# A two-layer attention trunk: readback of the transposed weights in a later step, and output blocks taken in another order

## The chip, the cores and the metric

The kernel runs on one core of a Trainium2 chip. The metric is the device time of one execution in microseconds (us), lower is better. One more execution was recorded by the hardware profiler; every row below is from it, with times counted from the start of its span. The granted clock of TensorE was 0.999 of full speed, which is the 2.4 GHz level, over the whole span.

## What is computed

256 tokens of width 2048 pass through two residual layers in float32. Layer a is multi-head latent attention, layer b is causal attention with ALiBi (its block selection has nothing to select at 256 tokens). Both have 16 heads of width 128, a gate, and an output projection. Cut to what matters:

```python
# layer a: h = rms_norm(x, norm_a)
proj = h @ w_in                        # 2048 -> 512 + 256 + 64 + 2048
q_lat, kv_lat, k_rope, gate = split(proj)
q  = rms_norm(q_lat) @ w_q_up          # 16 heads x (128 + 64 rotary)
kv = rms_norm(kv_lat) @ w_kv_up        # 16 heads x (128 key + 128 value)
q, k = rms_norm per head, rope on the rotary parts (one rotary key for all heads)
o = softmax(causal(q @ k.T * scale)) @ v
x = x + (o * silu(gate)) @ w_out_a     # 2048 -> 2048
# layer b: h = rms_norm(x, norm_b)
q, k, v, gate = split(h @ w_in_b)      # 4 x 2048
o = softmax(causal(rms_norm(q) @ rms_norm(k).T * scale - slope * distance)) @ v
x = x + (o * silu(gate)) @ w_out_b
```

## The kernel before

**Products.** A float32 product is made of three products of rounded halves: high by high, high by low, low by high. A weight tile (128 partitions by up to 1024 columns, `wr`, 512 KB) is loaded by SyncE's queue, its high half `wh` is made by ScalarE (L147), its low half `wl` by VectorE (L151), and TensorE multiplies (L199). There are four buffers of `wr`, four of `wh` and three of `wl`, taken in turn. TensorE's transposes are L202. Five of the eight banks of PSUM hold sums of blocks (`acc`), three serve the heads (`ps_s` for scores, `ps_o` for P·V, `ps_ta` for turned tokens, `ps_st` and `ps_r` for token statistics).

**Layer a.** After the latent projections, eight groups of two heads follow one another (`group_a`, L656 to L745), each with its part of w_q_up, of w_kv_up, and a gate block. A head is made of steps (`head_steps`, L450): the scores and softmax (`s1`: minimum L464, exponential L466, norm L469 and L471); the turning of the probabilities, which are split into two planes by ScalarE (L441), transposed by a DMA on SyncE's queue (L442), and put together again by VectorE, the *readback* (L448 in `flip`); their high half `ph` and low half `pl` (L490 and L493 on ScalarE, L491 on VectorE); and P·V (`s3`) with its gating L505 and the halves of the result, `ohl` (L506 on ScalarE, L507 on VectorE). If `away` is set, the turning stops behind the DMA, and the readback (L483) with the halves is a step of its own, later. Layer b's heads have `away=FLB` before and after the change.

The output projection of layer a is eight blocks of 256 columns, `outs_a`, each of 16 steps; step i needs head i. Blocks 0 to 3 use one bank and six matmuls of 256 columns a step, blocks 4 to 7 two banks and four matmuls (two of 512 and two of 256 columns). When a block ends, VectorE adds it to x (L406), ScalarE and VectorE split the new x (L333, L334) and sum its squares (L346, L348, L350, L351). Before that x and the causal mask's place in `c_sb` are loaded again (`reload`): four loads of xT and, last, the ALiBi distances, from which ScalarE makes each head's `alibi` tile in layer b (L883, L882 after the change).

**Layer b.** Four groups of four heads (`group_b`, L825), each with a gate (two blocks of 16 steps), q, k and v. Its token statistics are two small products, `ps_st` and `ps_r`; ps_r needs a diagonal from VectorE (L370).

**What sets the order.** `ordered` (L168) merges a main list (blocks of products) and a side list (head steps, turns, reloads). Each step has a planned cost, things it needs, and a lag behind them; a side step goes out as soon as its planned time has come. `run` then writes out the steps, with each load four weights ahead. Each engine works its instructions in order; a framework between the kernel and the engines may still set independent instructions of one engine in another order. TensorE's order is fixed by `chain`.

Of the kernel before, what the change touches and what calls it, by code (L numbers as in the profile page):

```python
# [31 lines left out]
NC = DM // P  # L32
# [12 lines left out]


PA, PB, LO, TU, TUB, S1, S2A, S2B, S3 = 9000, 6000, 5000, 3000, 10000, 4800, 6000, 9000, 3000
FLB = 4500
SLACK = 1.3
HOLD = 4500  # L50
PACE, PACEB = 600, 3500
# [42 lines left out]
def trunk(ctx: ExitStack, tc, xT, gains, cst, w_in_a, w_q_up, w_kv_up, w_out_a, w_in_b, w_out_b, outT):  # L94
    nc = tc.nc
# [422 lines left out]
    main, side = [], []  # L518
# [137 lines left out]
    def group_a(g):  # L656
# [65 lines left out]
        def scores(h):  # L722
            def f(ps):
                at = lambda x, i: [y[:, i] for y in x]
                products(ps, at(z["q"], h), at(z["k"], h), True)
                products(ps, at(z["r"], 0), at((krf,) + lat_st["kr"], h), False)
            return f
# [5 lines left out]
        for h in range(2):  # L733
            heads.append(head_steps(2 * g + h, scores(h), lambda: c_sb[:, C_MASK:C_MASK + 384],
                                    lambda h=h: [x[:, h] for x in z["v"]], 1090, turns + [kr], [], gates[g][-1:],
                                    S2A, nc.scalar.copy))
        proj[0].needs += lats
        if g > 1:
            proj[-1].after += turns_of[-2]
# [35 lines left out]
    def out_done_a(j):  # L775
        def f(a):
            xt = res["x"]
            c = 2 * j
            added(a, xt, c)
            split_x(c, G_NB)  # L780
            split_x(c + 1, G_NB)
            sum_squares(ssq_b, j)
        return f
# [9 lines left out]
    outs_a = [(blk_cols if j < 4 else blk_both)(w_out_a[:, 256 * j:256 * (j + 1)], og, out_done_a(j), 4000) for j in range(8)]  # L793

    for g in range(8):
        main += group_a(g)
        if g == 0:
            kr.after.append(main[-1])
        if g < 7:
            main += gates[g + 1][HALF:] + (gates[g + 2][:HALF] if g < 6 else [])  # L800
        gates[g][-1].after.append(row_a)
        if g > 3:
            gates[g][-1].after += [h[2] for h in heads[2 * g - 8:2 * g - 6]]
# [10 lines left out]
            outs_a[2 * j][-1].needs.append(again)  # L814
    for b in outs_a[:4]:
        main += b[:12]
    for b in outs_a[:4]:
        main += b[12:]
    main += sum(outs_a[4:], [])


    x_b = x_a
# [2 lines left out]
    def group_b(g):  # L825
# [49 lines left out]
        def scores(h):  # L875
            def f(ps):
                products(ps, [x[:, h] for x in z["Q"]], [x[:, h] for x in z["K"]], True)
            return f

        def bias(h):  # L880
            def f():
                b = wk.tile([P, 384], F32, tag="alibi", name="alibi", bufs=1)  # L882
                nc.scalar.activation(b, c_sb[:, C_MASK:C_MASK + 384], AF.Copy,  # L883
                                     scale=float(np.float32(2.0 ** (-8.0 * (h + 1) / H))))
                return b
            return f

        w = lambda i: w_in_b[:, DM * i + 512 * g:DM * i + 512 * (g + 1)]
        gate = []
# [9 lines left out]
        for h in range(4):  # L899
            hb.append(head_steps(4 * g + h, scores(h), bias(4 * g + h), lambda h=h: [x[:, h] for x in z["v"]],  # L900
                                 545, [tq, tk], v[-1:] + gate[-1:], [], S2B, nc.vector.tensor_copy, PACEB if g < 3 else PACE, FLB))
        for s in (gate[NC - 1], gate[-1]):
# [8 lines left out]
        turns_of.extend([[tq], [tk]])  # L911
        side.extend([tq, tk])
        side.extend(s for h in hb[-4:] for s in h)
        return gate + q + k + v

    def out_done_b(c0, m):
# [14 lines left out]
    for g in range(4):  # L931
        main += group_b(g)
# [66 lines left out]
```

## Time and profile before

| what | us |
|---|---|
| median of 3 runs | 754.15 (752.91 to 754.26) |
| the profiled execution | 752.38 |
| its span, first to last instruction | 750.6 |
| TensorE busy | 740.6 (99%) |
| VectorE busy | 589.5 (79%) |
| ScalarE busy | 491.3 (65%) |
| DMA, mean | 204 GB/s |

The table says how much of the span each engine worked. It does not say which wait matters; that is read from who waits for whom, from the chain of work that ended last, and from the timelines of single stretches. Layer a's groups lie between about 75 and 250 us, its output blocks end by 310 us, and layer b fills the rest.

### The profile page before, as it was taken

What the parts mean: (1) busy time and instruction counts of PE and PEld (TensorE: products, weight loads), DVE (VectorE), ACT (ScalarE), POOL (GpSimd) and SP (SyncE); (2) the same over time, 40 slices, a digit from 0 to 9 for tenths busy, and PEclk for the clock granted to TensorE, in tenths of its full rate; (3) what the DMA queues carried; (4) which work ended last, traced back from release to release, by engine and by line L of the source; (5) the groups of instructions that cost most, each with busy time, mean ns of one, the idle gap of its engine ahead of it and who ended that gap; (6) DMA issues with size and microseconds to landing.
All of it is one profiled execution on the core that took longest, in us unless ns stands there. A gap on an engine that the chain in (4) does not pass through costs nothing.

```text
span 750.6 us, 13198 instructions
## 1 busy us (share of the span) xinstructions
PE 740.6 (99%) x4766; PEld 689.4 (92%) x4766; DVE 589.5 (79%) x1244; ACT 491.3 (65%) x1041; POOL 0.2 (0%) x4
## 2 busy tenths in 40 slices
PE   8999999999999999999999999999999999999997
PEld 7999999999999989988889988898889988899997
DVE  6978899999998696775788867887787967878563
ACT  7767888888877575555666666675666766565441
POOL 0000000000000000000000000000000000000000
PEclk9999999999999999999999999999999999999999
DMA  9866666666666966667787868877779778867761
GB/s 301 268 177 183 169 185 162 180 177 153 189 180 180 294 196 221 198 181 210 222 223 210 205 197 225 230 201 205 208 227 220 200 212 223 215 214 201 249 221 49
DMA packets 150258, 153.13 MB, mean 204 GB/s; under 512 B 47280, under 2 KB 119344, under 8 KB 150192
## 3 DMA queue, kind: packets, MB, share of 16 engines
q1 hardware_dynamic: 150048, 152.27, 71.6%
q8 instruction: 37, 0.61, 0.3%
q14 instruction: 29, 0.24, 0.1%
q10 hardware_dynamic: 144, 0.02, 0.0%
HBM read 139.68 MB, written 2.10 MB: 189 GB/s over the span
## 4 chain that ended last, share of the span: by engine, by line
PE 90%; DVE 5%; DMA 2%; ACT 1%; issue 1%; SPq 0%; DVEq 0%; ACTq 0%
PE acc L199 83%; PE ps_s L199 4%; DVE wl L151 3%; PE ps_o L199 2%; PE ps_ta L202 1%; DMA c_sb<-cst 1%; DMA wr<-w_in_a 1%; ACT wh L147 1%; DMA sm<-pz 0%; DVE xt L406 0%; ACT sq L598 0%; ACT sf L584 0%; DVE rs_y L328 0%; DVE rs_t L327 0%; PE ps_lt L202 0%
## 5 line engine op out<-in xcount | busy, mean ns | idle before, releaser
L147 ACT ACTIVATE wh<-wr 128x1024 fp32r<-128x1024 f32 (+3 forms) x265 | 288.4, 1092 | 143.1 <-PE acc L199 116.6
L151 DVE TENSOR_TENSOR wl<-wr,wh 128x1024 fp32r<-128x1024 f32 (+3 forms) x265 | 314.1, 1189 | 72.3 <-PE acc L199 41.8
L199 PE MATMUL acc<-wh,xhl 128*128 128x512 f32 (+1 forms) x896 | 265.6, 375 | 0.9 <-ACT wh L147 0.9
L199 PEld LDWEIGHTS acc<-wh,xhl 128*128 128x128 f32 x896 | 169.0, 190 | 21.7 <-ACT wh L147 1.5
L199 PE MATMUL acc<-xhl,wh 128*128 128x256 f32 (+1 forms) x768 | 173.4, 313 | 0.0
L199 PE MATMUL acc<-ohl,wh 128*128 128x256 f32 (+1 forms) x800 | 172.2, 307 | 0.0
L199 PE MATMUL acc<-wl,xhl 128*128 128x512 f32 (+1 forms) x448 | 167.8, 375 | 0.8 <-DVE wl L151 0.8
L199 PE MATMUL acc<-ohl,wl 128*128 128x256 f32 x512 | 140.7, 275 | 0.6 <-DVE wl L151 0.6
L199 PE MATMUL acc<-xhl,wl 128*128 128x256 f32 x512 | 140.3, 274 | 0.0
L199 PEld LDWEIGHTS acc<-ohl,wh 128*128 128x128 f32 x800 | 130.1, 191 | 6.0
L199 PEld LDWEIGHTS acc<-xhl,wh 128*128 128x128 f32 x768 | 126.5, 191 | 6.5
L199 PEld LDWEIGHTS acc<-ohl,wl 128*128 128x128 f32 x512 | 98.4, 192 | 1.3 <-DVE wl L151 1.2
L199 PEld LDWEIGHTS acc<-xhl,wl 128*128 128x128 f32 x512 | 98.4, 192 | 0.2
L199 PEld LDWEIGHTS acc<-wl,xhl 128*128 128x128 f32 x448 | 85.0, 190 | 11.6 <-DVE wl L151 1.6
L199 PE MATMUL acc<-wh,xt 128*128 128x384 f32 (+1 forms) x192 | 57.3, 356 | 0.0
L466 ACT ACTIVATE sm<-sm,mn 128x128 f32<-128x128 f32 x64 | 29.1, 457 | 12.9 <-DVE mn L464 12.9
L199 PEld LDWEIGHTS acc<-wh,xt 128*128 128x128 f32 x192 | 35.1, 190 | 1.2
L199 PE MATMUL acc<-wl,xt 128*128 128x384 f32 (+1 forms) x96 | 33.6, 350 | 1.5 <-DVE wl L151 1.5
L406 DVE TENSOR_TENSOR xt<-acc,xt 128x256 f32<-128x256 f32 (+1 forms) x37 | 16.1, 484 | 14.1 <-PE acc L199 14.1
L490 ACT CAST ph<-pz 128x256 fp32r<-128x256 f32 x32 | 12.9, 403 | 18.8 <-DVE pz L483 10.6
L507 DVE TENSOR_TENSOR ohl<-og,ohl 128x256 fp32r<-128x256 f32 x32 | 13.5, 424 | 12.2 <-ACT ohl L506 11.7
L506 ACT ACTIVATE ohl<-og 128x256 fp32r<-128x256 f32 x32 | 13.8, 433 | 12.8 <-DVE og L505 12.7
(150 smaller groups left out, 724.9 us busy)
## 6 DMA issues: line engine op xcount, KB each, us to landing
wr<-w_in_b SPq DMA_DIRECT2D x128, 512.0 KB, 4.0
wr<-w_in_a SPq DMA_DIRECT2D x32, 512.0 KB, 4.1
wr<-w_out_a SPq DMA_DIRECT2D x32, 512.0 KB, 4.5
wr<-w_out_b SPq DMA_DIRECT2D x32, 512.0 KB, 4.4
wr<-w_in_a SPq DMA_DIRECT2D x15, 416.0 KB, 5.0
wr<-w_q_up SPq DMA_DIRECT2D x16, 384.0 KB, 3.8
wr<-w_kv_up SPq DMA_DIRECT2D x8, 512.0 KB, 4.0
xt<-xT SPq DMA_DIRECT2D x4, 512.0 KB, 5.2
```

The source lines that it names most:

```text
L147: nc.scalar.activation(self.ordering(self.h)[1], self.ordering(self.raw)[0], AF.Copy)
L151: nc.vector.tensor_tensor(self.ordering(self.l)[1], self.ordering(self.raw)[0], self.ordering(self.h.bitcast(F32))[1], op=ALU.subtract)
L199: chain(nc.tensor.matmul(*args, skip_group_check=True, **kw))
L202: chain(nc.tensor.transpose(*args))
L406: nc.vector.tensor_tensor(lines(y), unpaired(b[:, o:o + n]), lines(y), op=ALU.add)
L466: nc.scalar.activation(sm[:, sl], sm[:, sl], AF.Exp, bias=mn[:, t:t + 1], scale=-1.0, accum_out=rs[:, t:t + 1])
L490: nc.scalar.copy(ph, pz[:, :S])
L506: nc.scalar.activation(lines(ogh[:, h]), unpaired(og), AF.Copy)
L507: nc.vector.tensor_tensor(lines(ogl[:, h]), unpaired(og), lines(ogh[:, h].bitcast(F32)), op=ALU.subtract)
```

## The change

Three things. In groups 1 to 5 of layer a (heads 2 to 11) `away` is set to 4000, so that the planes are copied and transposed at a lag of 4000 behind the scores instead of 6000, and read back (L483) in a step of its own at a lag of 2000 behind that. The last four steps of output blocks 0 to 3, which stood together, are set between halves of blocks 4 and 5. In layer b's first group the first four steps of the second gate block are set before the last four of the first.

```diff
--- before.py
+++ after.py
@@ -45,7 +45,7 @@
 
 
 PA, PB, LO, TU, TUB, S1, S2A, S2B, S3 = 9000, 6000, 5000, 3000, 10000, 4800, 6000, 9000, 3000
-FLB = 4500
+FLA, FLB = 4000, 4500
 SLACK = 1.3
 HOLD = 4500
 PACE, PACEB = 600, 3500
@@ -733,7 +733,7 @@
         for h in range(2):
             heads.append(head_steps(2 * g + h, scores(h), lambda: c_sb[:, C_MASK:C_MASK + 384],
                                     lambda h=h: [x[:, h] for x in z["v"]], 1090, turns + [kr], [], gates[g][-1:],
-                                    S2A, nc.scalar.copy))
+                                    S2A, nc.scalar.copy, away=FLA if 0 < g < 6 else 0))
         proj[0].needs += lats
         if g > 1:
             proj[-1].after += turns_of[-2]
@@ -814,9 +814,8 @@
             outs_a[2 * j][-1].needs.append(again)
     for b in outs_a[:4]:
         main += b[:12]
-    for b in outs_a[:4]:
-        main += b[12:]
-    main += sum(outs_a[4:], [])
+    o = outs_a
+    main += o[0][12:] + o[4][:8] + o[1][12:] + o[4][8:] + o[2][12:] + o[5][:8] + o[3][12:] + o[5][8:] + o[6] + o[7]
 
 
     x_b = x_a
@@ -911,6 +910,8 @@
         turns_of.extend([[tq], [tk]])
         side.extend([tq, tk])
         side.extend(s for h in hb[-4:] for s in h)
+        if g == 0:
+            gate = gate[:12] + gate[NC:NC + 4] + gate[12:NC] + gate[NC + 4:]
         return gate + q + k + v
 
     def out_done_b(c0, m):
```

Rows of the instruction order are shown for three places. Numbers behind names tell buffers apart: `wl_3103` is the low half of the weight loaded as `wr_3099`.

VectorE around the readbacks of heads 10 (first `pz`) and 11 (second `pz`), before:

```order
L448 COPY pz_3015<-sm_2924 128x2x384
L151 TENSOR_TENSOR wl_3035<-wr_2991,wh_2993 128x768
L491 TENSOR_TENSOR pl_3020<-pz_3015,ph_3019 128x256
L394 TENSOR_TENSOR gx_3072<-acc_2734,rr_a_590 128x512
L151 TENSOR_TENSOR wl_3080<-wr_3031,wh_3033 128x1024
L448 COPY pz_3049<-sm_2950 128x2x384
L396 SCALAR_TENSOR_TENSOR gate_3071<-gate_3071,gx_3072 128x512
L151 TENSOR_TENSOR wl_3110<-wr_3076,wh_3078 128x1024
L491 TENSOR_TENSOR pl_3054<-pz_3049,ph_3053 128x256
L427 SCALAR_TENSOR_TENSOR sr0_3097<-ps_ta_3098,gq_a_119,sr0_3097 128x256
L151 TENSOR_TENSOR wl_3162<-wr_3106,wh_3108 128x1024
```

and after:

```order
L394 TENSOR_TENSOR gx_3058<-acc_2720,rr_a_590 128x512
L151 TENSOR_TENSOR wl_3066<-wr_3024,wh_3026 128x1024
L396 SCALAR_TENSOR_TENSOR gate_3057<-gate_3057,gx_3058 128x512
L483 COPY pz_3015<-sm_2924 128x2x384
L151 TENSOR_TENSOR wl_3103<-wr_3062,wh_3064 128x1024
L491 TENSOR_TENSOR pl_3084<-pz_3015,ph_3083 128x256
L427 SCALAR_TENSOR_TENSOR sr0_3090<-ps_ta_3091,gq_a_119,sr0_3090 128x256
L151 TENSOR_TENSOR wl_3162<-wr_3099,wh_3101 128x1024
L427 SCALAR_TENSOR_TENSOR sr0_3090<-ps_ta_3111,g_sb_70,sr0_3090 128x512
L483 COPY pz_3042<-sm_2950 128x2x384
L505 SCALAR_TENSOR_TENSOR og_3154<-ps_o_3149,gate_2361 128x256
L491 TENSOR_TENSOR pl_3144<-pz_3042,ph_3143 128x256
```

Head 10's readback moved behind a gate product, a weight's low half and the gate; head 11's readback and `pl` moved behind two more low halves and both L427 of the next group, and head 10's P·V result (L505) comes between.

ScalarE at the end of layer a, where `og_3763` is head 15 before:

```order
L147 ACTIVATE wh_3677<-wr_3675 128x1024 [waits DMAHW2_49,PE_49]
L147 ACTIVATE wh_3708<-wr_3706 128x1024 [waits DMAHW5_49,PE_49]
L506 ACTIVATE ohl_74<-og_3723 128x256 [waits DVE_49]
L147 ACTIVATE wh_3748<-wr_3746 128x1024 [waits DMAHW7_49,PE_49,Activation_49]
L506 ACTIVATE ohl_74<-og_3763 128x256 [waits DVE_49]
L883 ACTIVATE alibi_5151<-c_sb_71 128x384 [waits DMAHW3_49]
L147 ACTIVATE wh_3787<-wr_3785 128x1024 [waits DMAHW0_49,PE_49,Activation_49]
```

and after, where `og_3781` is head 15:

```order
L147 ACTIVATE wh_3747<-wr_3745 128x1024 [waits DMAHW6_49,PE_49]
L506 ACTIVATE ohl_74<-og_3741 128x256 [waits DVE_49]
L147 ACTIVATE wh_3787<-wr_3785 128x1024 [waits DMAHW0_49,PE_49,Activation_49]
L882 ACTIVATE alibi_5151<-c_sb_71 128x384 [waits DMAHW3_49]
L506 ACTIVATE ohl_74<-og_3781 128x256 [waits DVE_49]
L147 ACTIVATE wh_3826<-wr_3824 128x1024 [waits DMAHW2_49,PE_49,Activation_49]
```

The tile `alibi`, which waits for the reload of `c_sb`, stood behind the halves of head 15 (second L506) and now stands in front of them; one more `wh` went in front of both.

VectorE in the updates of the output blocks, where before `acc_3375`, `acc_3559` and `acc_3681` are blocks 1, 2 and 3:

```order
L406 TENSOR_TENSOR xt_3673<-acc_3375,xt_3673 128x512
L151 TENSOR_TENSOR wl_3867<-wr_3824,wh_3826 128x1024
L334 SCALAR_TENSOR_TENSOR xhl_73<-xt_3673,g_sb_70,xhl_73 128x256 x2
L350 TENSOR_TENSOR ssq_125<-ssq_125,sq_3859 128x256
L406 TENSOR_TENSOR xt_3673<-acc_3559,xt_3673 128x512
L351 TENSOR_TENSOR ssq_125<-ssq_125,sq_3859 128x256
L151 TENSOR_TENSOR wl_3907<-wr_3863,wh_3865 128x1024
L334 SCALAR_TENSOR_TENSOR xhl_73<-xt_3673,g_sb_70,xhl_73 128x256 x2
L350 TENSOR_TENSOR ssq_125<-ssq_125,sq_3898 128x256
L406 TENSOR_TENSOR xt_3673<-acc_3681,xt_3673 128x512
```

and after, where `acc_3830` and `acc_3831` are block 4 and `acc_3548` is block 2:

```order
L151 TENSOR_TENSOR wl_3937<-wr_3910,wh_3912 128x1024
L351 TENSOR_TENSOR ssq_125<-ssq_125,sq_3906 128x256
L406 TENSOR_TENSOR xt_3698<-acc_3830,xt_3698 128x256
L406 TENSOR_TENSOR xt_3698<-acc_3831,xt_3698 128x256
L406 TENSOR_TENSOR xt_3698<-acc_3830,xt_3698 128x256
L406 TENSOR_TENSOR xt_3698<-acc_3831,xt_3698 128x256
L151 TENSOR_TENSOR wl_3971<-wr_3933,wh_3935 128x1024
L334 SCALAR_TENSOR_TENSOR xhl_73<-xt_3698,g_sb_70,xhl_73 128x256 x2
L350 TENSOR_TENSOR ssq_125<-ssq_125,sq_3963 128x256
L406 TENSOR_TENSOR xt_3698<-acc_3548,xt_3698 128x512
```

Blocks 1, 2 and 3 were added one after the other; now block 4's four additions, a low half and block 4's split stand before the addition of block 2, whose bank block 5 takes next.

## Rows read from the trace of the kernel before

**Rows 1.** The page: busy time, share; a group: busy and mean ns | idle, releaser.

```profile
PE 740.6 (99%) x4766; PEld 689.4 (92%) x4766; DVE 589.5 (79%) x1244; ACT 491.3 (65%) x1041; POOL 0.2 (0%) x4
...
L490 ACT CAST ph<-pz 128x256 fp32r<-128x256 f32 x32 | 12.9, 403 | 18.8 <-DVE pz L483 10.6
```

**Rows 2.** Waits of TensorE, whole span: us in total, times, longest us.

```profile
PE acc L199 <- DVE wl L151: 2.9, 9, 0.6
```

**Rows 3.** TensorE's timeline, heads 10/11: start us, us, engine, line, shapes [idle before].

```profile
210.40 0.27 PE L199 MATMUL ps_o<-ph,vh 128*128 128x256 f32 x1
210.51 0.28 PE L199 MATMUL ps_o<-pl,vh 128*128 128x256 f32 x1
...
212.04 0.38 PE L199 MATMUL acc<-wh,xt 128*128 128x512 f32 x1
212.27 0.38 PE L199 MATMUL ps_o<-ph,vh 128*128 128x256 f32 x1
```

**Rows 4.** TensorE's timeline, kv_up of group 1.

```profile
123.97 0.46 PE L199 MATMUL acc<-wh,xt 128*128 128x512 f32 x1
124.70 0.48 PE L199 MATMUL acc<-wl,xt 128*128 128x512 f32 x1 [0.27 <-DVE wl L151]
```

**Rows 5.** The chain of waits, layer a: start us, us, what.

```profile
190.38 1.14 DVE wl L151
...
228.68 3.31 DMA sm<-pz
...
251.83 8.17 DMA c_sb<-cst
```

**Rows 6.** VectorE's timeline, heads 10 and 11.

```profile
209.16 0.61 DVE L448 COPY pz<-sm 128x768 uint16<-128x768 uint16 x1
...
211.39 0.42 DVE L491 TENSOR_TENSOR pl<-pz,ph 128x256 fp32r<-128x256 f32 x1
...
212.12 1.22 DVE L151 TENSOR_TENSOR wl<-wr,wh 128x1024 fp32r<-128x1024 f32 x1
213.26 0.75 DVE L427 SCALAR_TENSOR_TENSOR sr<-ps_ta,g_sb,sr 128x512 fp32r<-128x512 f32 x1
```

**Rows 7.** Waits of VectorE, 80 to 250 us: us in total, times, longest.

```profile
DVE pz L448 <- DMA sm<-pz: 4.2, 7, 1.4
```

**Rows 8.** TensorE's timeline, scores of head 14.

```profile
232.73 0.36 PE L199 MATMUL ps_s<-sr 128*128 128x256 f32 x1
233.31 0.51 PE L199 MATMUL ps_s<-sr 128*128 128x256 f32 x2 [0.22 <-DVE sr L427]
```

**Rows 9.** ScalarE's timeline, end of layer a.

```profile
256.10 0.43 ACT L506 ACTIVATE ohl<-og 128x256 fp32r<-128x256 f32 x1
260.02 0.52 ACT L883 ACTIVATE alibi<-c_sb 128x384 f32<-128x384 f32 x1 [3.49 <-DMA c_sb<-cst]
```

**Rows 10.** TensorE's timeline, blocks 0 and 4 of layer a's output.

```profile
257.20 0.39 PE L199 MATMUL acc<-ohl,wh 128*128 128x256 f32 x2
...
268.53 0.38 PE L199 MATMUL acc<-ohl,wh 128*128 128x512 f32 x1
269.20 0.38 PE L199 MATMUL acc<-ohl,wl 128*128 128x256 f32 x1 [0.29 <-DVE wl L151]
```

**Rows 11.** VectorE's timeline, block 0's update.

```profile
258.07 0.69 DVE L406 TENSOR_TENSOR xt<-acc,xt 128x512 f32<-128x512 f32 x1
```

**Rows 12.** VectorE's timeline, update of a block in two banks.

```profile
287.88 1.42 DVE L406 TENSOR_TENSOR xt<-acc,xt 128x256 f32<-128x256 f32 x4 [1.01 <-PE acc L199]
289.21 1.22 DVE L151 TENSOR_TENSOR wl<-wr,wh 128x1024 fp32r<-128x1024 f32 x1
290.34 0.88 DVE L334 SCALAR_TENSOR_TENSOR xhl<-xt,g_sb,xhl 128x256 fp32r<-128x256 f32 x2
```

**Rows 13.** TensorE's timeline, layer b's token statistics.

```profile
319.13 0.27 PE L199 MATMUL acc<-xhl,wl 128*128 128x256 f32 x1
319.88 0.81 PE L199 MATMUL ps_r<-diag,ones 128*128 128x256 f32 x2 [0.48 <-DVE diag L370]
```

## The prediction

> **What bounds the kernel now.** I read the busy times first: TensorE is busy 740.6 of 750.6 us [rows 1], so the time changes by what TensorE waits, and the change alters no product. Second come the waits of TensorE: VectorE's low halves of weights (wl, L151) hold it up 9 times, 2.9 us in all, 0.6 at most [rows 2]. That view counts only the empty time; what a wait costs is the start of a matmul less the start of the one before, less the normal spacing: 0.11 us for 256 columns (210.40 to 210.51) and 0.23 for 512 (212.04 to 212.27) [rows 3]. So the kv_up matmul at 124.70 is 124.70 - 123.97 - 0.22 = 0.51 us late [rows 4]. The chain of waits shows where else it happens: four such wl of layer a lie on it, up to 190.38, then a transpose that lands late at 228.68, then the reload of c_sb at 251.83 that takes 8.17 us [rows 5]. Each lost time below is read off TensorE's timeline by that subtraction.
>
> **The readback of heads 2 to 11.** Nothing is added: ten copies of 0.61 us [rows 6] become L483 in place of L448, and stand later in VectorE's queue. The front copy (L441) and the transpose are placed 2000 planned ns sooner (away 4000 against a lag of 6000), but SP's queue keeps its order of transposes and weight loads, and nothing new is queued behind a transpose there.
>
> Groups 1 to 4. VectorE's wl for kv_up stands behind two readbacks and two low splits (L491). Four matmuls wait for it, 0.51, 0.52, 0.51 and 0.58 us, 2.1 in all; the first is [rows 4], the chain shows the last [rows 5]. In the new order one readback and one split, 0.61 + 0.42 less an overlap of 0.2 [rows 6], go behind that wl. All 2.1 us would go if nothing else came late; but the second head's L491 now stands behind two wl of 1.22 us, and its first P·V matmul comes only six matmuls of kv_up later. By the durations that split ends 0.2 to 0.7 us after TensorE wants it, in three or four groups. I take -1.0, from -2.1 (no new wait) to +0.8 (0.7 in each group against 2.1).
>
> Group 5, heads 10 and 11. Here no matmul waited before, since VectorE just kept up: its timeline shows no idle time from 209 to 214 us (a wl takes 1.14 from its start to the next), and the second split ran at 211.39 for a matmul due at 212.27 + 0.2 [rows 3, 6]. In the new order the same instructions are laid end to end: gate product, wl, gate, L483 of head 10 at about 209.0, a wl of 1.14, L491 at 210.65 to 211.0. TensorE wants it at 210.51 [rows 3]: +0.5. Then L427, a wl, L427, and only then L483 of head 11, at about 213.15. ScalarE's L490 follows it (0.40 [rows 1]), and L491 ends near 214.6. TensorE, 0.5 later by then, wants it at 213.0: another 1.6 to 1.7. The step is **+2.2**; its ends are 0 (VectorE, which no longer stands 4.2 us at L448 for the landing of transposes [rows 7], has run ahead by that much, or more than needed) and +3.6 (ScalarE's L490, now behind one more weight's high half, is late by about the length of a wl as well). I take the laid-out value, since VectorE is full there.
>
> Head 14. At 232.73 the score matmul stands 0.47 us longer than it should (233.31 - 232.73 - 0.11) [rows 8], because VectorE waited at L448 for a transpose [rows 5], with L427 behind it. In the new order this head's scores come some 3 us later and that L448 is no longer in front of L427: **-0.5** (0 to -0.5).
>
> **The end of layer a's output.** Four things.
>
> Head 15's split waits for the reload. ScalarE stood 3.49 us at 260.02 before alibi (L883), until c_sb landed; L506 of head 15 had run just before, at 256.10 [rows 9], and step 15 of the first block, at 257.20 [rows 10], came 0.7 us after its end; L507, 0.43, lies between. In the new order TensorE does P·V of head 15 two microseconds later (18 matmuls of 0.11 move ahead of it), and in ScalarE's queue alibi (now L882) stands **ahead** of L506. If c_sb lands as before, L506 starts at 260.45, L507 ends at about 261.35, and the matmul of 257.20 waits 4.1 us, or 3.4 as TensorE comes 0.7 later by the terms so far. SP issues c_sb behind the weight load whose slot is freed by a wl; TensorE frees that wl's buffer by my count 1.4 us sooner now, and if half to all of that reaches the landing the wait is 2.0 to 2.7. I take the middle, **+2.3**, from 0 (c_sb lands before 255.5, that is within 5 us of its issue) to +4.1. The Trainium skill, "TensorE: Matmul & The Clock Gate", section "Architectural detail: the array is 16× 32×32, not 1× 128×128", has ScalarE's queue as strictly first in, first out. By that rule nothing lets L506 pass alibi; could it pass, this term would be 0 and the sum +1.1.
>
> Banks. Block 4 uses two PSUM banks, and the second is that of block 0, which ends directly before it. L406 takes 0.69 us, and began at 258.07 [rows 11], right behind the block's last matmul; TensorE has one step in the first bank, 0.33 us, to do meanwhile: +0.5 to +0.6. Block 5's second bank is block 2's, and VectorE now does four L406 of block 4 (1.42), a wl (1.14), two L334 (0.88) and an L350 before L406 of block 2: 3.4 us by [rows 12], some 0.3 for the L350, and 4.4 with L406 itself, against 24 matmuls (2.7) and 0.33 on TensorE: +1.3. Together **+1.9**, from 0.8 (one L406 each, less the first step) to 2.6.
>
> Block 4's late wl go. At 269.20, and again at 271.7, a wl is late, 269.20 - 268.53 - 0.22 = 0.45 each [rows 10], because ScalarE's wh stood behind alibi. In the new order the wh concerned precedes alibi, and three blocks' updates no longer come in a row: **-0.9** (0 to -0.9).
>
> **Layer b's gate.** The second statistics product (ps_r) waits 319.88 - 319.13 - 0.11 = 0.64 us for L370 [rows 13]. Sixteen matmuls, 2.6 us of the next block, now stand in front of it, and VectorE's order is the same: **-0.6**. The last steps of the first gate block move later by as much and nobody waits for them.
>
> **The sum.** -1.0 + 2.2 - 0.5 + 2.3 + 1.9 - 0.9 - 0.6 = +3.4 us. The profiled execution took 752.38 us (its span 750.6), so it would be 755.8; the median of the three runs is 754.15, 1.8 above, and I put the same difference on that: **757.5 us**. About 0.2%, 1.5 us, is what a measurement can tell from no change.
>
> **The rivals.**
>
> VectorE gets ahead (faster). The place is layer a from 80 to 250 us, where VectorE stood 4.2 us at L448, 7 times [rows 7]. If the later readback turns that into a lead, wl are early, and the lead covers group 5. It decides if VectorE has 2.2 us in hand at 205 us. Then the readback gives -2.1 - 0.5 and costs nothing; with -0.9 and -0.6 and low ends of the tail (0 and +0.8) the sum is -3.3: 750.8. For it: the copies do wait for landings now. Against it: VectorE had no idle time around heads 10 and 11, a stretch which had no such wait to win back. The Trainium skill, "DMA: Bandwidth & Descriptors", section "Rules for kernel authors", says to issue a DMA early, compute, and wait for it late, which is this edit; by it this rival would hold. The readback waits of [rows 7] agree with it, the order of group 5 does not.
>
> The reload lands early (no change). All as forecast but c_sb is there by 255.5, so head 15's split is on time: +1.1, 755.2. For it: the load is small, 128 by 384 words. Against: its 8.17 us [rows 5], behind the same loads of weights and xT as before.
>
> Both waits at their full size (slower still). Group 5 costs 3.6 and the reload 4.1, and the groups before gain nothing: 3.6 - 0.5 + 4.1 + 1.9 - 0.9 - 0.6 = +7.6, 761.7.
>
> That the readback is moved only in the text and not on VectorE is excluded by the order of its instructions.
>
> **How the numbers follow.** Forecast, between +1.5 and +5.5: 0.43. VectorE ahead: 0.24. Reload early, or its like with small terms: 0.26. Full size: 0.07. The range reaches down into the first rival, to 751.0, and up to 760.5, and leaves out most of the full size and the lower part of the first. Faster by over 0.2% is the first rival, 0.24; within it the second with a little of the forecast's lower edge, 0.27; slower 0.49.
>
> **What would show it.** Right: kv_up's matmuls near 124.7, 147, 169 and 191.6 without their gap, and small gaps at the second P·V; 0.5 and 1.6 us at the P·V of heads 10 and 11, with pl (L491) as the one waited for; ScalarE idle before alibi and L506 right behind it, with TensorE standing at the last matmuls of block 0; a gap behind the first step of blocks 4 and 5, released by L406; none at ps_r. Wrong: VectorE idle before L483 of head 10, or c_sb landing in under 5 us.

## The result, and the profile after

The changed kernel takes **760.16 us** (median of 4 executions, 760.01 to 761.35), the kernel before 754.2 beside it (4 executions, 752.91 to 756.16): a ratio of 1.0081 [1.0064, 1.0097], 0.8% slower. The forecast was 757.5, range 751.0 to 760.5.

The profiled execution of the changed kernel took 761.35 us, its span is 759.6. The one before had 750.6, so 9.0 us have to be found, 3 more than the medians differ by: the profiled execution before lay 1.8 below its median, this one 1.2 above. All four executions of the changed kernel list a mean granted clock of 0.995, against 0.999 in the profiled execution before.

The page of the changed kernel: busy time, share and instructions of each engine, and the granted clock of TensorE in 40 slices.

```profile
span 759.6 us, 13201 instructions
...
PE 744.0 (98%) x4766; PEld 691.6 (91%) x4766; DVE 588.7 (78%) x1244; ACT 490.8 (65%) x1041; POOL 0.2 (0%) x4
...
PEclk9999999999999989999999999999999999999999
```

TensorE has the same 4766 matmuls and is busy 3.4 us longer than in [rows 1]; one slice of its clock, the 15th (266 to 285 us), is an 8. So part of the loss is no wait at all. The waits of TensorE in the changed kernel (us in total, times, longest):

```profile
PE ps_o L199 <- ACT ph L490: 3.0, 2, 1.6
PE acc L199 <- ACT ohl L506: 2.5, 1, 2.5
...
PE ps_o L199 <- DVE pl L491: 1.4, 3, 0.6
...
PE acc L199 <- DVE wl L151: 1.2, 3, 0.6
```

The line of [rows 2], 9 waits for wl with 2.9 us, has shrunk to 3 with 1.2: the edit does what it says. But `ph`, `ohl` and `pl` have come in above it, and single waits for ScalarE's `ph` (1.6) and `ohl` (2.5) are longer than any wait for a wl was.

Counted as in the prediction (start to start of two matmuls, less the normal spacing), after against before:

| place | predicted us | measured us |
|---|---|---|
| groups 1 to 4: kv_up, and P·V instead | -1.0 | -1.5 |
| P·V of heads 10 and 11 | +2.2 | +3.0 |
| P·V of head 13 | not seen | +2.4 |
| scores of head 14 | -0.5 | -0.5 |
| halves of head 15, behind the reload | +2.3 | +3.0 |
| half clock behind that | not seen | +2.8 |
| bank, block 4 | +0.6 | +0.3 |
| bank, block 5 | +1.3 | 0 |
| late wl of block 4 | -0.9 | -0.9 |
| ps_r | -0.6 | -0.6 |
| first 103 us (loads, group 0) | 0 | +0.7 |
| sum | +3.4 | +8.7 |

The row on the first 103 us lies ahead of the first moved head: up to there TensorE's order is the same in every kernel of this document, and the traces differ all the same (a matmul of layer a's ps_r that starts at 46.06 us before starts at 46.51 after and at 48.20 in experiment e2 below). The others, one by one.

**Heads 10 and 11.** VectorE's timeline of the changed kernel (start, us, line, shapes, [idle before, releaser]) and then TensorE's:

```profile
208.74 0.60 DVE L483 COPY pz<-sm 128x768 uint16<-128x768 uint16 x1
...
210.35 0.41 DVE L491 TENSOR_TENSOR pl<-pz,ph 128x256 fp32r<-128x256 f32 x1
...
212.99 0.59 DVE L483 COPY pz<-sm 128x768 uint16<-128x768 uint16 x1
...
214.62 0.43 DVE L491 TENSOR_TENSOR pl<-pz,ph 128x256 fp32r<-128x256 f32 x1 [0.73 <-ACT ph L490]
```

```profile
212.66 0.38 PE L202 MATMUL ps_ta<-c_sb,ra 128*128 128x128 f32 x2
214.64 0.38 PE L199 MATMUL ps_o<-ph,vh 128*128 128x256 f32 x1 [1.59 <-ACT ph L490]
215.10 0.38 PE L199 MATMUL ps_o<-pl,vh 128*128 128x256 f32 x1
```

Head 11's readback begins at 212.99 where the prediction had laid it at 213.15, and its `pl` begins at 214.62 where the prediction had it end. At head 11 TensorE waits for `ph` first, and not for `pl`: ScalarE's L490 begins at 214.17, 0.6 us after the readback's end, behind short instructions of the next group (L421, L666, L668). The wait is 1.8, with 0.35 more at the `pl` behind it; at head 10 the wait is 0.8, for `pl`.

**Head 13.** This one the prediction did not have. SyncE's queue, VectorE and TensorE of the changed kernel:

```profile
230.88 1.59 SPq L442 DMA_TRANSPOSE sm<-pz  x1
```

```profile
236.74 0.60 DVE L448 COPY pz<-sm 128x768 uint16<-128x768 uint16 x1 [2.86 <-DMA sm<-pz]
```

```profile
236.20 0.28 PE L199 MATMUL acc<-ohl,wl 128*128 128x256 f32 x1
237.88 0.38 PE L199 MATMUL ps_o<-ph,vh 128*128 128x256 f32 x1 [1.41 <-ACT ph L490]
```

Heads 12 and 13 are not in the edit; their planes still come back at L448. But TensorE's order has changed around them: P·V of heads 12 and 13 now stands before the scores of heads 14 and 15. VectorE stands 2.86 us for a transpose that was issued at 230.88 and is there some 5.8 us later, and TensorE, which has nothing in between, stands too: 1.6 at `ph` and 0.8 at `pl`. Before, the transpose issued at 230.58 was read at 235.18, 4.6 us later, and the scores of heads 14 and 15 stood in front of that P·V.

**Head 15.** ScalarE of the changed kernel, then TensorE:

```profile
263.32 0.52 ACT L882 ACTIVATE alibi<-c_sb 128x384 f32<-128x384 f32 x1 [3.14 <-DMA c_sb<-cst]
263.75 0.41 ACT L506 ACTIVATE ohl<-og 128x256 fp32r<-128x256 f32 x1
```

```profile
261.44 0.28 PE L199 MATMUL acc<-ohl,wl 128*128 128x256 f32 x1
264.21 1.04 PE L199 MATMUL acc<-ohl,wh 128*128 128x256 f32 x2 [2.50 <-ACT ohl L506]
```

In [rows 9] L506 ran at 256.10 and alibi waited behind it. Now L506 runs right behind alibi, and TensorE stands 2.66 us for it and 0.35 for L507's half. The load of c_sb was issued at 256.52 and was there at 263.3, in 6.8 us; the 8.17 of [rows 5] came down by 1.4. Its issue moved by 4.7 us, from 251.83, and TensorE's last step of block 0, at 257.20 in [rows 10] and due at 261.55 here, by 4.3.

**The half clock.** TensorE's granted clock behind that stand, in stretches of the changed kernel (columns: stretch and its us, then busy us (instructions) of PE, PEld, DVE, ACT and POOL, granted clock, DMA share, GB/s):

```profile
261.50:264.20 2.70, 0.21 (x2) 0.02 (x1) 0.01 (x1) 0.84 (x2) 0.00 (x0) 1.00 0.85 272
264.20:266.00 1.80, 1.73 (x7) 1.52 (x8) 0.42 (x1) 0.02 (x1) 0.00 (x0) 0.56 0.06 21
266.00:268.00 2.00, 1.86 (x6) 1.26 (x6) 1.85 (x3) 2.00 (x4) 0.00 (x0) 0.50 0.00 0
268.00:270.00 2.00, 2.00 (x7) 1.68 (x7) 1.10 (x3) 0.36 (x1) 0.00 (x0) 0.50 0.40 120
270.00:272.00 2.00, 2.00 (x10) 1.75 (x9) 0.40 (x1) 0.46 (x1) 0.00 (x0) 0.69 0.40 142
272.00:274.00 2.00, 2.00 (x14) 1.84 (x13) 0.83 (x1) 0.60 (x1) 0.00 (x0) 1.00 0.01 3
```

The columns of PE and of the clock tell it: TensorE works 0.21 of 2.70 us while it stands, and for the 7 us after that it is busy nearly all the time, but with 6 or 7 instructions in two microseconds instead of 14, at a granted clock of 0.50, the 1.2 GHz level. From 265.05 to the end of block 4's first half at 274.02 it takes 8.97 us; in experiment e4 below, which has TensorE's order unchanged and no such stand, the same matmuls take 6.41. Of these 8.97 a bank wait is 0.34, of the 6.41 it is 0.62, so the low clock cost 8.63 - 5.79 = 2.8 us: about as much again as the stand.

### The profile page after: what moved, and what is told of

It reads as the page before. It is cut to its first block, busy times and chain, and to the rows that moved or that the text cites. A ratio compares the mean times of both kernels' runs of the same rounds, so it can differ in the third digit from the quotient of the medians.

```text
span 759.6 us, 13201 instructions
## 1 busy us (share of the span) xinstructions
PE 744.0 (98%) x4766; PEld 691.6 (91%) x4766; DVE 588.7 (78%) x1244; ACT 490.8 (65%) x1041; POOL 0.2 (0%) x4
## 4 chain that ended last, share of the span: by engine, by line
PE 65%; DVE 0%; issue 0%
PE acc L199 62%; PE ps_s L199 1%; PE ps_o L199 1%; DVE xt L406 0%; PE ps_r L199 0%; PE ps_st L199 0%; DVE ohl L507 0%
## 5 line engine op out<-in xcount | busy, mean ns | idle before, releaser
L199 PE MATMUL acc<-ohl,wh 128*128 128x256 f32 (+1 forms) x800 | 175.3, 310 | 2.7 <-ACT ohl L506 2.5
L406 DVE TENSOR_TENSOR xt<-acc,xt 128x256 f32<-128x256 f32 (+1 forms) x37 | 16.1, 483 | 18.2 <-PE acc L199 18.2
L490 ACT CAST ph<-pz 128x256 fp32r<-128x256 f32 x32 | 12.9, 404 | 23.7 <-DVE pz L483 14.0
L507 DVE TENSOR_TENSOR ohl<-og,ohl 128x256 fp32r<-128x256 f32 x32 | 13.5, 424 | 17.1 <-ACT ohl L506 17.0
L506 ACT ACTIVATE ohl<-og 128x256 fp32r<-128x256 f32 x32 | 13.7, 432 | 14.6 <-DVE og L505 14.6
```

What stands on the lines that cost most here:

```text
L199: chain(nc.tensor.matmul(*args, skip_group_check=True, **kw))
L406: nc.vector.tensor_tensor(lines(y), unpaired(b[:, o:o + n]), lines(y), op=ALU.add)
L490: nc.scalar.copy(ph, pz[:, :S])
L506: nc.scalar.activation(lines(ogh[:, h]), unpaired(og), AF.Copy)
L507: nc.vector.tensor_tensor(lines(ogl[:, h]), unpaired(og), lines(ogh[:, h].bitcast(F32)), op=ALU.subtract)
```

## The experiments

The theory behind e1 to e3 was that the readback alone carries the loss, with alibi's place as part of it; the rival, that the order of blocks puts alibi ahead of head 15's halves. Each median stands beside that of the kernel before, taken with it on the same chip.

**One part alone.** e1 has the readback only, e2 the order of blocks only, e3 the gate only.

```diff
e1:
-                                    S2A, nc.scalar.copy))
+                                    S2A, nc.scalar.copy, away=FLA if 0 < g < 6 else 0))
e2:
-    for b in outs_a[:4]:
-        main += b[12:]
-    main += sum(outs_a[4:], [])
+    o = outs_a
+    main += o[0][12:] + o[4][:8] + o[1][12:] + o[4][8:] + o[2][12:] + o[5][:8] + o[3][12:] + o[5][8:] + o[6] + o[7]
e3:
+        if g == 0:
+            gate = gate[:12] + gate[NC:NC + 4] + gate[12:NC] + gate[NC + 4:]
```

> The kernel before with the readback of heads 2 to 11 alone. Theory: every loss comes from this edit, the position of alibi ahead of head 15's L506 too, so it is slower than the whole change without the gains of the other two edits: 754.2 - 1.5 + 3.0 - 0.5 + 2.4 (heads 13 and 12) + 3.0 (head 15 behind the reload) + about 3 (half clock behind that stand) = about 763, at least 760; alibi's wait for the reload stands before L506. Rival: the reload's wait at head 15 comes from the new order of the output blocks; then only the terms of heads 10 to 13 and the groups are seen, 757 to 758, and no half clock.

> The kernel before with the new order of the output blocks alone. Theory: block 4's two late low halves go (-0.9), a bank wait of 0.3 to 0.6 behind block 0 comes: 753.7 to 754.0, no half clock. Rival: this order brings the reload's wait at head 15 and the half clock, 759 to 760.

> The kernel before with the interleaved gate blocks alone. Theory: the 0.64 us at ps_r goes and nothing else moves: 753.6, within what can be told from no change. Rival: the late end of the first gate block costs as much: 754.2.

| kernel | us | before | ratio |
|---|---|---|---|
| e1, readback | 758.62 | 754.03 | 1.0077 [1.0047, 1.0107] |
| e2, blocks | 753.28 | 754.03 | 0.9990 [0.9976, 1.0005] |
| e3, gate | 752.91 | 754.03 | 0.9984 [0.9969, 0.9999] |

The whole loss is the readback's. In e1's trace the waits of heads 10 and 11 (0.83, 1.80 and 0.35) and of head 13 (0.98 and 0.84) are there, and so is the stand at head 15: 1.96 us in front of the matmul at 263.34, with alibi ahead of L506. In e2 there is no such stand, and alibi runs behind L506. So the prediction, which has alibi's place under the end of layer a's output, together with what the order of blocks does, had it beside the wrong edit. The median of e1 lies lower than its theory had it, near the figure that the rival gave, so here the trace decides between them and not the time. e2 shows the bank wait of block 4, 0.62 us, and its late wl gone; e3 has no wait at ps_r.

e1 also tells where the low clock falls. Its windows, behind the stand of head 11 (1.80 us) and behind that of head 15 (1.96 us):

```profile
216.00:217.00 1.00, 1.00 (x5) 0.82 (x4) 0.48 (x1) 1.00 (x6) 0.00 (x0) 0.50 0.02 8
217.00:218.00 1.00, 1.00 (x7) 1.00 (x7) 1.00 (x3) 1.00 (x4) 0.00 (x0) 0.50 0.00 0
```

```profile
264.00:266.00 2.00, 2.00 (x19) 2.00 (x19) 1.34 (x2) 1.41 (x3) 0.00 (x0) 1.00 0.04 12
```

In this execution the clock fell behind the first and not behind the second; in the changed kernel's it was the other way, 1.00 in every stretch from 208 to 220 us, after the same 1.8 us wait at head 11. The low clock of e1 cost 1.7 us: from 213.85 to 219.41 its matmuls take 5.57 us, and the same matmuls 3.90 in experiment e7 below, where the clock stayed up there.

**Alibi's place alone.** e4 is the whole change with alibi held behind the halves of head 15; e8 is the kernel before with alibi put in front of them.

```diff
e4, against the changed kernel:
-            nc.scalar.activation(lines(ogh[:, h]), unpaired(og), AF.Copy)
+            hi = nc.scalar.activation(lines(ogh[:, h]), unpaired(og), AF.Copy)
+            if h == H - 1 and "last" not in res:
+                res["last"] = hi
...
+                if h == 0:
+                    after(ins, res["last"])
e8, against the kernel before (alibi of head 0 made here, used in layer b):
+            if h == H - 1 and "last" not in res:
+                res["last"] = hi
...
+                res["first"] = nc.scalar.activation(b, c_sb[:, C_MASK:C_MASK + 384], AF.Copy,
+                                                    scale=float(np.float32(2.0 ** (-8.0 / H))))
+                behind(res["last"], res["first"])
```

> The changed kernel, with alibi put behind head 15's L506 on ScalarE. Theory: the stand of 2.7 us at block 0's last step goes, and the half clock behind it, about 3 us, with it: 754 to 755 (760.2 - 6). Rival A: the stand goes but the half clock has another cause: 757. Rival B: L506 waits for the weight ahead of it anyway and nothing changes: 760.

> The kernel before with nothing but alibi put ahead of head 15's L506 on ScalarE. Theory: TensorE stands at block 0's step 15 from 257.2 until c_sb has landed (260.0) and two copies are done, 3 to 4 us, less the two late low halves of block 4 (0.9); with the clock kept 756.5, and 759 to 760 if it falls to half behind the stand, as in the changed kernel. Rival: the reload lands sooner if less is in its way and the stand is under 1 us: 754.5.

e4, beside e1 to e3: 755.3 us, ratio 1.0028 [1.0012, 1.0044]; the changed kernel's median less this is 4.9 us. ScalarE and TensorE of e4:

```profile
259.06 0.44 ACT L506 ACTIVATE ohl<-og 128x256 fp32r<-128x256 f32 x1 [0.60 <-DVE og L505]
...
261.27 0.52 ACT L884 ACTIVATE alibi<-c_sb 128x384 f32<-128x384 f32 x1 [1.77 <-DMA c_sb<-cst]
```

```profile
260.90 0.27 PE L199 MATMUL acc<-ohl,wl 128*128 128x256 f32 x1
261.63 0.48 PE L199 MATMUL acc<-ohl,wh 128*128 128x512 f32 x1 [0.46 <-DVE xt L406]
```

No wait for `ohl` is left, the granted clock of this execution is 1.000 over the span, and the next thing to show is block 4's second bank, 0.62 us, waiting for L406 as predicted.

e8: 759.1 us beside 753.96, ratio 1.0061 [1.0038, 1.0084], and its executions lie in two clusters, near 757.5 and near 760.4. ScalarE, TensorE and the windows behind it, in the kernel before with nothing but this instruction moved (L774 and L508 are alibi and the high half of head 15):

```profile
261.07 0.52 ACT L774 ACTIVATE alibi<-c_sb 128x384 f32<-128x384 f32 x1 [3.90 <-DMA c_sb<-cst]
261.50 0.41 ACT L508 ACTIVATE ohl<-og 128x256 fp32r<-128x256 f32 x1
```

```profile
258.56 0.28 PE L199 MATMUL acc<-ohl,wl 128*128 128x256 f32 x1
261.96 0.38 PE L199 MATMUL acc<-ohl,wh 128*128 128x256 f32 x1 [3.13 <-ACT ohl L508]
```

```profile
262.00:263.00 1.00, 0.92 (x3) 0.72 (x4) 1.00 (x2) 0.86 (x1) 0.00 (x0) 0.67 0.00 0
263.00:264.00 1.00, 1.00 (x7) 1.00 (x6) 0.60 (x2) 0.27 (x1) 0.00 (x0) 0.50 0.00 0
...
265.00:266.00 1.00, 1.00 (x8) 1.00 (x7) 1.00 (x2) 1.00 (x3) 0.00 (x0) 0.63 1.05 366
266.00:268.00 2.00, 2.00 (x20) 2.00 (x19) 1.31 (x4) 0.64 (x2) 0.00 (x0) 1.00 0.67 227
```

One copy of 0.52 us, set ahead of another in ScalarE's queue, stops TensorE for 3.3 us and brings the low clock with it, here for a shorter time: the matmuls from 262.80 to 266.00 take 3.20 us, and the same ones 1.79 in the kernel before. The trace is of an execution of the lower cluster (757.89), so the low clock alone doesn't tell the clusters apart; but the mean granted clocks are 0.996 to 0.998 in the lower and 0.992 to 0.995 in the higher one, so the higher one had more of it, somewhere in the span. Alibi's place is the largest single item of the change, and nothing in the diff names it.

**Which groups.** e5 has the readback in groups 1 to 4 only, e7 in group 5 only, e6 is the whole change with groups 1 to 4.

```diff
e5 and e6, against the readback as changed:
-    away=FLA if 0 < g < 6 else 0
+    away=FLA if 0 < g < 5 else 0
e7:
-    away=FLA if 0 < g < 6 else 0
+    away=FLA if g == 5 else 0
```

> The kernel before with the readback moved in groups 1 to 4 alone (heads 2 to 9). Theory: four late low halves of kv_up, 2.1 us, go, 0.6 comes back at P·V of second heads, and nothing behind group 4 moves: 754.0 - 1.5 = 752.5. Rival: the later readback disturbs the heads behind it whichever group it is in: 756 to 757, with waits at heads 12 and 13 and at head 15.

> The whole change with group 5 left as before. Theory: the gains of all three edits stand without the losses: 754.0 - 1.5 - 0.9 + 0.6 - 0.6 = 751.6, faster than before by 0.2 to 0.4%. Rival: the edits' gains don't add, since one takes the slack that another used: 753 to 754.

> The kernel before with the readback moved in group 5 alone (heads 10 and 11). Theory: this carries the whole loss of the first edit, so it is slower than the run with all five groups by the 1.5 us that groups 1 to 4 gave: 758.6 + 1.5 = 760, with 3.0 us at heads 10 and 11, about 2 at head 13 and 2 to 3 at head 15. Rival: part of it comes from groups 1 to 4: 757 or less.

| kernel | us | before | ratio |
|---|---|---|---|
| e7, group 5 | 761.24 | 753.96 | 1.0093 [1.0063, 1.0122] |
| e5, groups 1 to 4 | 755.72 | 753.96 | 1.0013 [1.0000, 1.0027] |
| e6, whole change, groups 1 to 4 | 754.29 | 753.96 | 0.9999 [0.9984, 1.0015] |

Group 5 alone has everything that made the change slow: in e7's trace heads 10 and 11 wait 0.53, 1.80 and 0.35, head 13 1.45 and 0.84, head 15 2.49 and 0.35, the clock is 0.91 and 0.67 in the windows behind, TensorE's order is that of the changed kernel up to the output blocks, and ScalarE has alibi ahead of L506. The 0.53 at head 10, where the changed kernel has 0.83, shows a side effect: the time won in groups 1 to 4 brings TensorE to head 10 sooner, and some of it is lost there.

The expectations of e5 and e6 were missed: four kv_up waits go, 2.1 us, and yet no gain comes out. Their traces show why. VectorE of e5, then TensorE, at heads 10 and 11, which e5 doesn't move:

```profile
209.91 0.61 DVE L448 COPY pz<-sm 128x768 uint16<-128x768 uint16 x1 [1.78 <-DMA sm<-pz]
```

```profile
212.66 0.48 PE L199 MATMUL acc<-wl,xt 128*128 128x512 f32 x1 [1.05 <-DVE wl L151]
...
214.79 0.38 PE L199 MATMUL ps_o<-ph,vh 128*128 128x256 f32 x1 [0.79 <-DVE sr L427]
...
237.82 0.38 PE L199 MATMUL ps_s<-xt,sr 128*128 128x256 f32 x1 [1.39 <-DVE sr L427]
```

The framework now put L448 of head 11 right behind the split of head 10, ahead of a wl. It stood 1.78 us for its transpose, issued at 203.85, with that wl, the gate and L427 queued behind it. TensorE lost 1.3 and 0.95 us here and 1.56 at the last score matmul of head 14, by the same pattern at a later L448. The four waits won were paid back at the first group that was left as it was, and more at head 14.

**A border further forward, and another lag.** If the loss is that of the first unmoved group behind a moved one, it should depend on which group that is. e10 is the whole change with groups 1 to 3, e11 with groups 1 to 4 and FLA 5000, e9 has the blocks and the gate without any readback.

```diff
e10:
-    away=FLA if 0 < g < 6 else 0
+    away=FLA if 0 < g < 4 else 0
e11:
-FLA, FLB = 4000, 4500
+FLA, FLB = 5000, 4500
-    away=FLA if 0 < g < 6 else 0
+    away=FLA if 0 < g < 5 else 0
e9, against the changed kernel:
-    S2A, nc.scalar.copy, away=FLA if 0 < g < 6 else 0))
+    S2A, nc.scalar.copy))
```

> The kernel before with the second and third edit, without the readback edit. Theory: both gains add, since they lie 50 us apart: 754.0 - 0.9 + 0.6 - 0.6 = 753.1, or 752.2 by the medians that each gave alone (-0.75 and -1.1). Rival: one uses the other's slack and nothing is left: 754.0.

> The whole change with the readback moved in groups 1 to 3 alone. By the order of VectorE's instructions, group 4 then takes the disturbance that group 5 had with groups 1 to 4 (the second readback directly behind the first one's split), and group 5 stands as before. Theory: the loss at the next group comes from that place in the order only; group 4 has no score of an output block behind it and loses at most 0.6, as group 0 does: three late wl go (-1.5), 753.1 - 1.5 = 751.6. Rival: the group behind the last moved one always loses what group 5 lost (1.3 + 0.95): 753.9 or more.

> The whole change with the readback moved in groups 1 to 4 and a lag of 5000 instead of 4000, by which VectorE's order of group 5 on is that of before. Theory: no loss at group 5, but the splits of both heads stand behind both low halves of the moved groups, and the first head's P·V comes late by about a wl (1.1) in each of four groups: 753.1 - 2.1 + 4 = 755. Rival: TensorE's blocks cover that and the four late wl just go: 751.0.

| kernel | us | before | ratio |
|---|---|---|---|
| e9, blocks and gate | 752.71 | 753.5 | 0.9979 [0.9965, 0.9993] |
| e10, whole change, groups 1 to 3 | **750.67** | 753.5 | 0.9969 [0.9954, 0.9983] |
| e11, groups 1 to 4, FLA 5000 | 756.17 | 753.5 | 1.0030 [1.0015, 1.0045] |

e10 is faster than both kernels (its profiled execution, 752.39 us, is one of its slower ones, with a granted clock of 0.52 between 12 and 15 us, at the first loads). VectorE at the first unmoved group behind the moved ones (group 4), and the waits of TensorE in e10:

```profile
186.92 0.61 DVE L448 COPY pz<-sm 128x768 uint16<-128x768 uint16 x1 [0.42 <-DMA sm<-pz]
```

```profile
PE acc L199 <- DVE wl L151: 1.7, 5, 0.6
...
PE acc L199 <- DVE xt L406: 0.5, 1, 0.5
```

The transpose has nearly landed by the time VectorE is at L448 (0.42 us of idle time, against 1.78 in e5), group 4's kv_up waits 0.61 as it did before, three other kv_up waits are gone, the halves of head 15 come ahead of alibi, and of the tail only block 4's bank is left. How much of e10's gain beyond e9, 2 us, is the readback's is not settled: the two intervals overlap, and in the traces e10 wins 1.0 us on e9 between 103 and 213 us (three waits gone, 0.43 and 0.16 at P·V of second heads come) and loses 0.3 at the scores of head 14. It also lacks a late wl at 250 us that e9 has with 0.92 and the kernel before has not.

In e11 the copies come closer to the readback, and TensorE waits at the first P·V of every moved group; the first one:

```profile
125.18 0.33 PE L199 MATMUL acc<-wh,xt 128*128 128x384 f32 x1
126.22 0.38 PE L199 MATMUL ps_o<-ph,vh 128*128 128x256 f32 x1 [0.71 <-ACT ph L490]
```

It is 0.72 to 0.87 late there and 0.89 at the `pl` behind it, four times: 6.6 us, against 2.1 won at kv_up. The idle times of group 5 that e5 and e6 had are not there. So the lag has its own price: with this one each moved group loses 1.6 us, over twice what the prediction had as the upper bound for a late second split at a lag of 4000.

## Why the prediction came out as it did

The sign was right, and so was the mechanism of two of the three large terms (heads 10 and 11, head 15); of the third, the banks, only block 4's came, and two effects of over 2 us each were missing. The time was 2.7 us too low, at the upper end of the range. That it lies in the range at all is partly luck: from profile to profile the prediction had 755.8 and 761.35 came, 5.6 more. Some 3 us of that vanish in the medians because of which executions were profiled, and the 1.6 us of bank waits that didn't come stand against the missing terms.

- **Groups 1 to 4** were sized nearly right (-1.0, measured -1.5): of the "three or four" late splits only two came, 0.45 and 0.17 us. (The upper end, +0.8, is 0.7 by its own figures: four times 0.7 less 2.1.)
- **Heads 10 and 11** are the step in which laying the instructions end to end paid. The readbacks came within 0.3 us of their places, the end of head 11's split 0.45 later. The term was 0.8 too small: 0.3 at head 10, where TensorE came 0.5 sooner than the term had it, and 0.5 at head 11, mostly since ScalarE's L490 was given no wait of its own. Such a wait was in the upper bound, though for one more weight's high half, and not for the short instructions that stood directly in front.
- **Head 13** is the step that was missing. The prediction looked at what the moved heads' instructions pass, and did not ask what TensorE meets next when the planner's whole order shifts: P·V of heads 12 and 13 in front of the scores of heads 14 and 15, with a transpose that lands in 5.8 us. Every run with group 5 moved has this wait (e1, e4, e7), and none of the others; which part the order has in it and which the slow transpose, no run tells apart. The step "Head 14: -0.5" spoke of that very shift, and took only its gain.
- **Head 15 behind the reload** had the mechanism, its place and its wait (2.66 and 0.35 against 2.3 forecast). The step of it that fell is the cause: it is group 5's readback that sets alibi ahead, not the order of blocks, as e1, e2 and e7 show. The size came near by another way than the prediction's: it had the load of c_sb issued up to 1.4 us sooner against TensorE, but the issue went 0.4 us later than TensorE's step did (4.7 against 4.3), and what shortened the wait is that the load took 6.8 us and not 8.17.
- **The half clock** was no term at all. The prediction priced every wait by its length; this one cost 2.8 us more, the largest of the missing terms.
- **The banks.** Block 4 as said (0.62 in e2 and e4; 0.34 in the changed kernel, where L406 had more time at the low clock). Block 5's 1.3 us was a misreading: its second bank isn't block 2's, as the text ahead of the prediction had it. Block 5 starts to fill it before block 2 is added. TensorE and VectorE of the changed kernel:

```profile
284.95 0.38 PE L199 MATMUL acc<-ohl,wh 128*128 128x512 f32 x1
```

```profile
285.41 0.68 DVE L406 TENSOR_TENSOR xt<-acc,xt 128x512 f32<-128x512 f32 x1
```

- **Late wl of block 4** and **ps_r** came as forecast (-0.93 and -0.64; the second late wl stood at 272.40, not at 271.7). The second, where [rows 13] had a gap of 0.48, in the changed kernel:

```profile
331.53 0.27 PE L199 MATMUL acc<-xhl,wl 128*128 128x256 f32 x1
331.64 0.71 PE L199 MATMUL ps_r<-diag,ones 128*128 128x256 f32 x2
```

**The rivals.** *VectorE gets ahead* did not come: the waits for transposes in layer a went from 7 with 4.2 us in [rows 7] to 3 with 5.1, so the time was not won but gathered at fewer places, one of them on the path. VectorE in the changed kernel, 80 to 250 us:

```profile
DVE pz L448 <- DMA sm<-pz: 5.1, 3, 2.9
```

The rule of the Trainium skill that the prediction weighed ("DMA: Bandwidth & Descriptors", "Rules for kernel authors": issue early, wait late) held where TensorE had other work while the readback came later (groups 1 to 3 in e10), and not where it wanted that readback's result next (heads 10 and 11). *The reload lands early* fell: 6.8 us. *Both at full size*, 761.7, was near the number, by other terms.

**What stays open.** Why the transposes of heads 11 (e5) and 13 take about 6 us to be there was not measured by itself, nor why the framework sets alibi ahead of L506 when group 5 moves; the edit touches neither instruction. The runs also don't tell which stands bring the low clock: it followed 2.66 us, 2.49 (e7) and 3.29 (e8), it followed 1.80 in e1 and not in the changed kernel, and it did not follow 1.96 in e1. Part of what separates executions of one kernel is a low clock elsewhere: the traces of e2, e5, e7, e10 and e11 have it between 11 and 16 us, at the first loads, and those of the kernels before and after have not; at 60 us e5 is 2.1 us behind the kernel before, whose TensorE order it shares.

## What to carry to other kernels

When a step is moved later, lay out every in-order queue again up to the next stage, and not only around the moved step: most of the loss stood at heads 13 and 15 (2.4, and 5.8 with the low clock), which the edit doesn't name; at head 13 TensorE's order had changed, at head 15 ScalarE's. An instruction that waits for a load belongs behind everything that is already due on its engine; e4 and e8 show what one such place is worth, about 5 us of 754 either way. And move by groups: with no group moved the other two edits gained 0.2%, with three groups the whole change gained 0.3%, with four nothing, and with the fifth it lost 0.8%.

## What the runs showed of the hardware

A stand of TensorE cost more than its length where the clock fell behind it: 2.66 us in the changed kernel, then 7 us at granted clocks of 0.50 to 0.69, for another 2.8 us; 3.29 us in e8, and then 0.50 to 0.67 until 266 us, for 1.4 us or more on top. In e1 the fall came behind heads 10 and 11 instead, 0.50 from 215 to 218 us, for 1.7 us. The Trainium skill, "TensorE: Matmul & The Clock Gate", section "HAM oscillation — how this bites in real kernels", describes waits for data that throw TensorE back to its lower level; these rows agree, with a single wait in the middle of a kernel that is 98% busy.
